# Queries and keys of one attention group as Strassen products, made before the pairs and loaded

## The chip, the cores and the metric

The kernel runs on one core of a Trainium2 chip, in a single launch. The metric is the device time of one execution in microseconds; the lower, the better. The time before is the median of three runs.

## The reference

A decoder trunk of two layers over x of 1024 rows and 1024 columns, in float32. The first layer is dilated sliding-window attention; the change touches only how its queries and keys are made. The second is a state-space layer (S5) with its own projections, a scan, and a gated linear unit.

```python
def dilated_attention_mixer(h, w_in, w_out, rel_bias):
    proj = h @ w_in
    qkv = proj[..., :n_qkv].reshape(B, S, 3, N_GROUPS_A, ATTN_HEADS, HEAD_DIM)
    z = proj[..., n_qkv:]
    for g, (window, dilation) in enumerate(DILATED_GROUPS):   # (128, 1), (512, 4), (2048, 16)
        o, l = dilated_group_attention(qkv[:, :, 0, g], qkv[:, :, 1, g], qkv[:, :, 2, g],
                                       rel_bias, window, dilation)
        ...
    wts = jax.nn.softmax(jnp.stack(lses), axis=0)
    o = jnp.sum(wts[..., None] * jnp.stack(outs), axis=0)
    return (o * jax.nn.silu(z)) @ w_out
```

There are 16 heads of 64 columns and three groups. Each group has its own queries, keys and values, so the input projection has 3 x 3 x 1024 columns and another 1024 for the gate.

## The kernel before, in words

Every large product is made of three TensorE matmuls: each operand is split into a high part (a float32r copy, made by ScalarE's cast) and a low part (the difference, made by VectorE or GpSimd), and high x high, high x low and low x high are added in PSUM. `split` does that; the tiles whi and wlo are the parts of a weight, hh and hl those of the normed input h, kept in SBUF as two halves of 512 rows.

**The values stage** (`v_phase`). The normed input is made and transposed. Chunk 0 of the values is a direct product (`first_values`). The other five chunks go through `Quads`: the input's four quarters (two halves of rows, two of the inner dimension) and their Strassen-Winograd sums are made once (`self.rows`), and each chunk of weights is cut in four quarters. `quad` runs seven products instead of eight: for each it makes the weight combination on VectorE (line 300), splits it, runs the matmuls, and adds the result into sums in SBUF (lines 337 to 348). Products that share an accumulator follow one another in one PSUM bank set (`ACC`). One product of the values is 48 matmuls with 256 moving columns (line 371). The results are stored to a DRAM tensor, v_dr. Between products, jobs for the second layer's tables run (`Prep.powers`, `Prep.products`), each after a given count of products, `q.jobs`: for table et of eight, powers after product 8 + 3 et and products after 10 + 3 et. Powers builds two tables in the two buffers of the ring wraw, and they stay there until products has used them.

**The pairs** (`attention`, `attn_pair`). Eight pairs of heads follow. In each, for each of the three groups, the query and then the key weights (128 columns each) are loaded (`load_w`, line 95) through the ring wraw, split into the rings whi and wlo (two buffers each; here GpSimd makes the low part, line 84), and multiplied with the two halves of h (`proj_half`, line 110: 24 matmuls of 128 x 512 each, into one of two PSUM banks psj). `evac_q` and `evac_k` split each result from PSUM into qh, ql, kh and kl, reordered so that the rows of a residue class of the dilation lie together. Each of these has a ring of two buffers, so group n + 2 takes the buffers of group n. Then `attn_unit` runs twice: scores (line 469) into psl, of which there is one, scaled bias and row maximum on VectorE (line 475), exponentials on ScalarE (line 486), transposes on TensorE (line 497), a split, and the product with the values vs (lines 546, 572). GpSimd merges the three outputs of the pair before and makes rotation tables for the second layer (`rotations`).

The rest is the attention's gate and output projection, the second layer with its projections, the gated linear unit, and the last projection.

The order of instructions on each engine is set at build time by a scheduler that knows dependencies and a model of costs; `high_priority(AHEAD)` lets an instruction go ahead of those emitted up to 600 places earlier. On the chip each engine runs its queue in that order. All DMAs of this kernel are issued from SP's queue.

Of the kernel before, what the change touches and what calls it, by code (L numbers as in the profile page):

```python
# [23 lines left out]
P = 128  # L24
S = 1024
# [2 lines left out]
H = 512  # L28
NEG = -1.0e30
EPS = 1e-6  # L30

AHEAD = 600

# [208 lines left out]
class Quads:  # L242
# [4 lines left out]
    def __init__(self, c):  # L247
        nc = c.nc
        self.c = c

        def part(th, kh):
            return [t[:, 4 * kh:4 * kh + 4, :] for t in c.h[th]]

        add, sub = ALU.add, ALU.subtract

        def tt(o, x, y, op):
            nc.vector.tensor_tensor(o, x, y, op=op)

# [24 lines left out]
        t2, t3 = c.vslot(2, F32), c.vslot(3, F32)  # L283
        self.sums = [t2[:, 0:2], t2[:, 2:4], t3[:, 0:2]]
        self.tmp = t3[:, 2:4].rearrange("p a x -> p (a x)")


    done, jobs = 0, {}

    def quad(self, raw, order, product, banks, use):  # L290

        c, nc = self.c, self.c.nc
        b11, b12, b21, b22 = raw
        n = b11.shape[2]
        tmp = self.tmp[:, 0:4 * n].rearrange("p (k x) -> p k x", k=4)
# [24 lines left out]

        accs = [None] * 3
        for i in order:
            w = weights(i)
            if accs[ACC[i]] is None:
                accs[ACC[i]] = banks(ACC[i])
            acc = accs[ACC[i]]
            product(i, self.rows[i], w, acc)
            self.done += 1  # L330
            for job in self.jobs.get(self.done, ()):
                job()
            with c.tc.high_priority(AHEAD):
                for b, ps in enumerate(acc):
                    p1, u2, u3 = (self.at(s, b) for s in self.sums)
                    if i == 0:
                        nc.scalar.copy(p1, ps)
                    elif i == 1:
                        t = c.slot("c11", tag="a")
                        nc.scalar.copy(t, ps)  # L340
                        use(0, 0, b, t)
                    elif i == 5:
                        nc.vector.tensor_tensor(u2, p1, ps, op=ALU.add)
                    elif i == 6:
                        nc.vector.tensor_tensor(u3, p1, ps, op=ALU.add)
                    else:
                        t, th, nh = {4: (u3, 1, 1), 3: (p1, 1, 0), 2: (u2, 0, 1)}[i]
                        nc.vector.tensor_tensor(t, t, ps, op=ALU.add)
                        use(th, nh, b, t)
# [30 lines left out]
        self.quad(quarters, [0, 1, 5, 6, 4, 3, 2], product, banks, use)  # L380


def gates(c, a, h, es):

    nc = c.nc
# [14 lines left out]
def v_phase(c, a, rows):  # L400
# [107 lines left out]
def out_tile(c, g, O):  # L508

    if not c.compact:  # L510
        c.compact = [c.outs.tile([64] + s, F32, name=f"cm{n}")
                     for n, s in enumerate(([3, 2, 32], [3, 32], [2, 32]))]
    if len(O) == g:
        O.append(c.outs.tile([P, S], F32, tag="O", name=f"O{g}", bufs=4))
    return O[g]


# [118 lines left out]
    return w  # L636


def attn_pair(c, p, w_in, h):
    nc = c.nc  # L640
    c.pair = p
    O = []
    for g in range(3):
        qh = c.attn.tile([P, S], F32R, tag="qh", name="qh", bufs=2)
        ql = c.attn.tile([P, S], F32R, tag="ql", name="ql", bufs=2)
        w = load_w(c, w_in[g * 8 + p])
        for th in range(2):
            src = proj_half(c, w, h[th])
            with c.tc.high_priority(AHEAD):
                evac_q(c, src, g, th * H, (qh, ql))  # L650
        bt = load_bias(c, p, g)
        kh = c.attn.tile([P, S], F32R, tag="kh", name="kh", bufs=2)
        kl = c.attn.tile([P, S], F32R, tag="kl", name="kl", bufs=2)
        w = load_w(c, w_in[(3 + g) * 8 + p])
        for th in range(2):
            src = proj_half(c, w, h[th])
            with c.tc.high_priority(AHEAD):
                evac_k(c, src, g, th * H, (kh, kl))
        v = load_v(c, p, g)
        rotations(c, p, g)  # L660
        if g == 1:
            run_merge(c)
        ms = c.small.tile([P, 32], F32, tag="ms", name="ms")
        for u in range(2):
            attn_unit(c, g, u, (qh, ql), (kh, kl), v, bt, ms, O)
            if p and g == u == 0:
                merge_weights(c, p - 1)
    if p == 7:
        merge_weights(c, p)
# [440 lines left out]
class Prep:  # L1110
# [4 lines left out]
    def __init__(self, c, a, v):  # L1115
        nc = c.nc
        self.c, self.a = c, a
        O = []
        o = [out_tile(c, c_, O) for c_ in range(4)]
# [319 lines left out]
def trunk(tc, a):  # L1439
# [4 lines left out]
    with ExitStack() as es:  # L1444
# [15 lines left out]
        dram = lambda name, shape: c.dr.tile(shape, F32, name=name)  # L1460
        c.vec_dr = dram("vec_dr", [3, 16, 384])
        c.v_dr = dram("v_dr", [3, 2, S, H])
        c.ms_dr = dram("ms_dr", [8, 3, 4, S])
        c.wt_dr = dram("wt_dr", [8, 3, 2, S])
        c.on_dr = dram("on_dr", [8, P, S])
# [139 lines left out]
```

## Time and profile before

| | |
|---|---|
| median of 3 runs | 1699.68 us (1697.64 to 1700.20) |
| profiled execution | 1703.36 us, span 1701.6 us, granted clock 0.992 |
| TensorE busy (PE) | 1651.8 us, 97% of the span, 9710 matmuls |
| TensorE weight loads (PEld) | 1399.3 us |
| VectorE (DVE) | 1012.8 us, 60% |
| ScalarE (ACT) | 711.9 us, 42% |
| GpSimd (POOL) | 461.6 us, 27% |
| DMA | 212.72 MB, mean 125 GB/s |

Busy time is the union of an engine's instruction times. A matmul's time in the profile reaches over the start of the next one, so TensorE's share says that it had work, and the distance from start to start says what a matmul costs. A row of a group of instructions has its line, engine, operation, tiles (written <- read) and shapes, its count, busy us and mean ns, and then the engine's idle time just before it and what ended that. In a timeline the idle time stands in brackets at the end of a row. A row of waits has the waiting engine and line, what it waited for, us in total, times and the longest. SPq is SP's DMA queue.

### The profile page before, as it was taken

Reading aid. Unit: us, or ns where it says so; the run is one execution under the profiler, and the core shown is the slowest. Engines: PE = TensorE matmul, PEld = TensorE weight load, DVE = VectorE, ACT = ScalarE, POOL = GpSimd, SP = SyncE. Lnnn points to the kernel's source line nnn. Section 1 sums busy time; section 2 is a strip of 40 time slices with the busy share of each in tenths; the row PEclk is TensorE's granted clock in tenths of the full one; section 3 lists DMA queues with packets and bytes.
Section 4 is the critical chain, followed back from the end, with each engine's and each line's share of the span. In section 5 each row is a group of like instructions: output and inputs, shape, how many; then the busy total and the mean of one; then the engine's idle time right before and its main releaser. Section 6 shows DMA issues by size and latency. Waiting matters only on the chain. (4 is left out here: it accounts for less than half of the span.)

```text
span 1701.6 us, 26274 instructions
## 1 busy us (share of the span) xinstructions
PE 1651.8 (97%) x9710; PEld 1399.3 (82%) x9710; DVE 1012.8 (60%) x2501; ACT 711.9 (42%) x1728; POOL 461.6 (27%) x303
## 2 busy tenths in 40 slices
PE   6999999999999999999999999998998999979998
PEld 5889999988888888888888888887887888868886
DVE  7698898725455455555455454558462777765533
ACT  5232232226556454645546464654452232233411
POOL 2000000041242513324161532404220444423121
PEclk9999999999999999999999999998999999999999
DMA  6223465352232323223242323428249765455432
GB/s 236 92 52 106 138 178 160 106 160 63 66 102 80 107 64 107 73 81 99 70 130 67 111 82 93 122 63 215 95 139 251 219 211 213 144 183 170 148 118 87
DMA packets 176901, 212.72 MB, mean 125 GB/s; under 512 B 37361, under 2 KB 133380, under 8 KB 176772
## 3 DMA queue, kind: packets, MB, share of 16 engines
q1 hardware_dynamic: 176772, 211.04, 41.4%
q8 instruction: 76, 1.25, 0.3%
q14 instruction: 53, 0.43, 0.1%
HBM read 154.03 MB, written 56.96 MB: 124 GB/s over the span
## 5 line engine op out<-in xcount | busy, mean ns | idle before, releaser
L110 PE MATMUL psj<-hh,whi 128*128 128x512 f32 x896 | 359.7, 401 | 3.4 <-DVE tz L784 3.4
L110 PE MATMUL psj<-hh,wlo 128*128 128x512 f32 x896 | 359.6, 401 | 0.0
L110 PE MATMUL psj<-hl,whi 128*128 128x512 f32 x896 | 356.3, 398 | 0.0
L84 POOL TENSOR_TENSOR wlo<-wraw,whi 128x1024 fp32r<-128x1024 f32 x48 | 115.2, 2399 | 392.7 <-ACT whi L83 329.1
L110 PEld LDWEIGHTS psj<-hh,whi 128*128 128x128 f32 x896 | 169.7, 189 | 40.4 <-DVE tz L784 3.8
L110 PEld LDWEIGHTS psj<-hh,wlo 128*128 128x128 f32 x896 | 169.5, 189 | 36.8 <-POOL wlo L84 0.3
L110 PEld LDWEIGHTS psj<-hl,whi 128*128 128x128 f32 x896 | 169.6, 189 | 36.3
L486 ACT ACTIVATE lg<-lg,nm 128x128 f32<-128x128 f32 (+1 forms) x384 | 168.2, 443 | 36.3 <-DVE nm L481 36.3
L83 ACT CAST whi<-wraw 128x1024 fp32r<-128x1024 f32 x80 | 83.7, 1047 | 195.6 <-PE psj L110 133.9
L475 DVE CUSTOM_DVE_ANT_0 lg<-psl,T 128x128 f32<-128x128 f32 (+1 forms) x384 | 110.6, 347 | 89.8 <-PE psl L469 89.8
L110 PE MATMUL psj<-h1h,whi 128*128 128x512 f32 (+1 forms) x272 | 106.0, 390 | 10.3 <-DVE z L1385 8.8
L371 PE MATMUL psq<-whi,v 128*128 128x256 f32 x640 | 115.9, 281 | 0.0
L84 DVE TENSOR_TENSOR ph<-pt,ph 128x512 fp32r<-128x512 f32 (+2 forms) x160 | 96.8, 623 | 15.5 <-ACT ph L83 13.4
L110 PE MATMUL psj<-h1h,wlo 128*128 128x512 f32 (+1 forms) x272 | 104.4, 385 | 0.0
L110 PE MATMUL psj<-h1l,whi 128*128 128x512 f32 (+1 forms) x272 | 104.2, 383 | 0.0
L84 DVE TENSOR_TENSOR kl<-psj,kh 128x512 fp32r<-128x512 f32 x48 | 33.2, 692 | 117.2 <-ACT kh L83 116.7
L83 ACT CAST ph<-pt 128x512 fp32r<-128x512 f32 (+2 forms) x160 | 81.6, 530 | 46.4 <-PE pt L497 45.3
L371 PEld LDWEIGHTS psq<-whi,v 128*128 128x128 f32 x640 | 98.6, 189 | 1.0 <-ACT whi L83 0.6
L371 PE MATMUL psq<-wlo,v 128*128 128x256 f32 x320 | 90.0, 282 | 2.2 <-DVE wlo L84 2.2
L546 PE MATMUL pso<-ph,vs 128*128 128x256 f32 (+1 forms) x544 | 86.5, 284 | 0.0
L1201 POOL TENSOR_TENSOR Ks<-Ks,O 32x64 f32<-32x64 f32 x8 | 4.6, 574 | 296.5 <-ACT Ks L1199 280.8
L497 PE MATMUL pt<-identr,lg 128*128 128x128 f32 x560 | 82.2, 277 | 0.0
(278 smaller groups left out, 3700.4 us busy)
## 6 DMA issues: line engine op xcount, KB each, us to landing
wraw<-in_w_in_dram SPq DMA_DIRECT2D x56, 512.0 KB
mw<-wt_dr SPq DMA_DIRECT2D x48, 256.0 KB
v<-in_w_v_dram SPq DMA_DIRECT2D x20, 512.0 KB
vp<-v_dr SPq DMA_DIRECT2D x16, 512.0 KB
wraw<-in_ssm_w_in_dram SPq DMA_DIRECT2D x16, 512.0 KB
v_dr<-v SPq DMA_DIRECT2D x30, 256.0 KB
rot_dr<-rt SPq DMA_DIRECT2D x48, 128.0 KB
ca_dr<-ca SPq DMA_DIRECT2D x32, 144.0 KB
```

What stands on the lines that cost most here:

```text
L83: nc.scalar.copy(hi, src)
L84: return (engine or nc.vector).tensor_tensor(lo, src, f32(hi), op=ALU.subtract)
L110: nc.tensor.matmul(ps, a[:, s], b[:, k, :], start=first and k == 0 and n == 0, stop=k == KT - 1 and n == 2, skip_group_check=True)
L371: nc.tensor.matmul(o, r[x][:, k, ts], w[y][:, k, :], skip_group_check=True, start=i in (0, 4, 5) and t % 2 == k == n == 0, stop=k == 3 and ...
L475: nc.vector.tensor_tensor_reduce(lg[:, h, j, 0:w], psl[:, h, o], bt[:, h, 256 - w:256], scale=1.0, scalar=-3.0e38, op0=ALU.add, op1=ALU.ma ...
L486: nc.scalar.activation(lg[:, h, j, 0:w], lg[:, h, j, 0:w], AF.Exp, bias=nm[:, h, b:b + 1], accum_out=ms[:, col:col + 1])
L497: c.nc.tensor.transpose(pt[:, n * P:(n + 1) * P], lg[:, h, j, part * P:part * P + P], c.ident)
L546: nc.tensor.matmul(o, l, r, start=n == 0, stop=n == len(jobs) - 1, skip_group_check=True)
L1201: nc.gpsimd.tensor_tensor(Ks[:, :, 0:16], Ks[:, :, 0:16], self.dd, op=ALU.add)
```

## The change

The queries and keys of the group with dilation 4 (g = 1) are no longer projected within the pairs. For each of the eight pairs, a new quad runs at the end of `v_phase`, behind the values. Its weights are the pair's 128 query columns and 128 key columns side by side, so that one half of the Strassen columns gives the queries and the other the keys. Its products have the weights as the stationary operand: 12 matmuls of 128 x 512 each. The raw weights alternate between two slots of the values stage, as do the sums (`self.turn`). Each result is split into its high and low part, reordered as the evacuation did it, and stored to a new DRAM tensor, qk_dr. The split parts stand in a buffer of the ring wraw, for the last two pairs in the ring b. In a pair the second group loads its four tiles from qk_dr into the buffers of the rings qh, ql, kh and kl.

The table jobs come after products 8 + 5 et and 11 + 5 et. `GROUPS` gives the order of the groups in a pair, which stays 0, 1, 2; `rotations`, `run_merge` and the merge's weights are called by place in that order.

```diff
+GROUPS = ((0, 1, 2), (0, 1, 2))
+MADE = [(p, 1) for p in range(8)]
...
+def halves(c, last, src, scale=None):
+    if last:
+        hi, lo = (c.slot(x, F32R, tag="b") for x in ("qkh", "qkl"))
+    else:
+        t = c.wraw.tile([P, 2, H], F32R, tag="wraw", name="qks")
+        hi, lo = t[:, 0], t[:, 1]
+    hi, lo = (x.rearrange("p (r l) -> p r l", r=src.shape[1]) for x in (hi, lo))
+    split(c, hi, lo, src, scale)
+    return hi, lo
+
+def put_qk(c, i, th, nh, t):
+    p, g = MADE[i]
+    o = ORD[g]
+    n = H // o
+    src, scale, at = t.rearrange("p (l r) -> p r l", r=o), None, th * n
+    if nh == 0:
+        src, scale, at = src[:, :, ::-1], 0.125, (1 - th) * n
+    for x, v in enumerate(halves(c, i >= len(MADE) - 2, src, scale)):
+        off = c.qk_dr.offset + ((i * 2 + nh) * 2 + x) * P * S + at
+        c.nc.sync.dma_start(bass.AP(c.qk_dr.tensor, off, [[S, P], [S // o, o], [1, n]]), f32(v))
...
+    def tiles(self, srcs, use):
+        c, nc = self.c, self.c.nc
+        self.turn ^= 1
+        raw = c.vslot(10 + self.turn, F32).rearrange("p (n a) x -> p n (a x)", n=2)
+        for n, s in enumerate(srcs):
+            nc.sync.dma_start(raw[:, n], s)
...
+        def product(i, r, w, acc):
+            for k in range(4):
+                for n, (x, y) in enumerate(((0, 0), (0, 1), (1, 0))):
+                    nc.tensor.matmul(acc[0], w[x][:, k, :], r[y][:, k, :], skip_group_check=True,
+                                     start=i in (0, 4, 5) and k == n == 0, stop=k == 3 and n == 2)
...
+        self.quad(quarters, [0, 5, 1, 6, 4, 3, 2], product, banks, lambda th, nh, b, t: use(th, nh, t))
...
-        q.jobs.setdefault(8 + 3 * et, []).append(lambda et=et: prep.powers(et))
-        q.jobs.setdefault(10 + 3 * et, []).append(lambda et=et: prep.products(et))
+        q.jobs.setdefault(8 + 5 * et, []).append(lambda et=et: prep.powers(et))
+        q.jobs.setdefault(11 + 5 * et, []).append(lambda et=et: prep.products(et))
     for ch in range(2, 6):
         q.values(a, ch)
+    for i, (p, g) in enumerate(MADE):
+        q.tiles([a["w_in"][(3 * x + g) * 8 + p] for x in range(2)],
+                lambda th, nh, t, i=i: put_qk(c, i, th, nh, t))
...
+def queries_keys(c, p, g, w_in, h):
+    q, k = ([c.attn.tile([P, S], F32R, tag=x + y, name=x + y, bufs=2) for y in "hl"] for x in "qk")
+    if (p, g) in MADE:
+        for n, ts in enumerate((q, k)):
+            for x, t in enumerate(ts):
+                c.nc.sync.dma_start(f32(t), c.qk_dr[MADE.index((p, g)), n, x])
+        return q, k
+    for n, (ts, evac) in enumerate(((q, evac_q), (k, evac_k))):
+        w = load_w(c, w_in[(3 * n + g) * 8 + p])
...
+    for n, g in enumerate(GROUPS[p % 2]):
+        q, k = queries_keys(c, p, g, w_in, h)
```

More of the change, by code (lines that the diff above doesn't have):

```diff
@@ L285, in __init__ @@
         self.tmp = t3[:, 2:4].rearrange("p a x -> p (a x)")
+        self.turn = 0
     done, jobs = 0, {}
@@ L380, in values, with banks @@
         self.quad(quarters, [0, 1, 5, 6, 4, 3, 2], product, banks, use)
+    def tiles(self, srcs, use):
[4 more added lines that the diff above has]
+            nc.sync.dma_start(raw[:, n], s)
+        raw = raw.rearrange("p n (k x) -> p n k x", k=KT)
+        quarters = [raw[:, nh, 4 * kh:4 * kh + 4] for kh in range(2) for nh in range(2)]
+        def banks(n):
+            pool, tag = ((c.psj, "psj"), (c.psl, "psl"), (c.pso, "pso"))[n]
+            return [pool.tile([P, H], F32, tag=tag, name="psq")]
+        def product(i, r, w, acc):
[3 more added lines that the diff above has]
+                                     start=i in (0, 4, 5) and k == n == 0, stop=k == 3 and n == 2)
+        turn = self.turn
+        self.at = lambda s, b: s[:, turn]
+        self.quad(quarters, [0, 5, 1, 6, 4, 3, 2], product, banks, lambda th, nh, b, t: use(th, nh, t))
 def gates(c, a, h, es):
@@ L649, in attn_pair @@
             with c.tc.high_priority(AHEAD):
-                evac_q(c, src, g, th * H, (qh, ql))
-        bt = load_bias(c, p, g)
[L652 to L658, printed above, removed]
+                evac(c, src, g, th * H, ts)
+    return q, k
+def attn_pair(c, p, w_in, h):
+    c.pair = p
+    O = {}
+    for n, g in enumerate(GROUPS[p % 2]):
+        q, k = queries_keys(c, p, g, w_in, h)
+        bt = load_bias(c, p, g)
         v = load_v(c, p, g)
-        rotations(c, p, g)
-        if g == 1:
+        rotations(c, p, n)
+        if n == 1:
             run_merge(c)
@@ L664, in attn_pair @@
         for u in range(2):
[L665 to L666 removed]
+            attn_unit(c, g, u, q, k, v, bt, ms, O)
+            if p and n == u == 0:
                 merge_weights(c, p - 1)
@@ L1117, in __init__ @@
         self.c, self.a = c, a
-        O = []
-        o = [out_tile(c, c_, O) for c_ in range(4)]
+        O = {}
+        o = [out_tile(c, n, O) for n in range(4)]
         def table(t, at, w):
```

15 lines of the change are left out of this document (4 added, 11 removed).

## The prediction

> **What bounds the kernel now.** I read the page's engine totals first, then the stretches, TensorE's waits, and the timeline. The columns of a stretch are its length, busy us and instruction count of each engine, the granted clock, the DMA share and GB/s. 113 to 343 us is the values stage, 343 to 1170 us the eight pairs, 560 to 657 us one pair.
>
> ```profile
> PE 1651.8 (97%) x9710; PEld 1399.3 (82%) x9710; DVE 1012.8 (60%) x2501; ACT 711.9 (42%) x1728; POOL 461.6 (27%) x303
> ...
> 113.00:343.00 230.00, 226.18 (x1882) 217.53 (x1881) 190.94 (x411) 62.12 (x96) 9.79 (x16) 1.00 0.44 135
> 343.00:1170.00 827.00, 823.61 (x4967) 684.55 (x4966) 421.66 (x1289) 438.11 (x1259) 281.48 (x150) 1.00 0.34 96
> ...
> 560.00:657.00 97.00, 97.00 (x598) 80.83 (x597) 49.50 (x158) 52.48 (x154) 34.38 (x18) 1.00 0.31 87
> ```
>
> TensorE is busy without a break in both stages; VectorE has 83% of the values stage (190.9 of 230 us) and about half of a pair. The two views of TensorE's waits, of the values stage and of 345 to 1160 us, have little:
>
> ```profile
> PE psq L371 <- DVE wlo L84: 3.0, 2, 2.2
> ...
> PE psj L110 <- DVE tz L784: 3.4, 1, 3.4
> ```
>
> So time taken off TensorE comes off the span, as long as its cover holds. But a busy matmul overlaps the next, so its price is not the 401 ns of its row but the distance of starts. The first projections of the pairs run 99 matmuls unbroken, from the first to the last of these:
>
> ```profile
> 344.20 0.39 PE L110 MATMUL psj<-hh,whi 128*128 128x512 f32 x1
> ...
> 366.97 0.39 PE L110 MATMUL psj<-hl,whi 128*128 128x512 f32 x1
> ...
> 345.00:365.00 20.00, 20.00 (x88) 16.23 (x87) 1.00 0.66 196
> ```
>
> 22.77 us over 98 distances is 0.2324 us; 20 us over the 87 weight loads gives 0.230. I use 0.2324.
>
> The Trainium skill, "TensorE: Matmul & The Clock Gate", section Back-to-back issue gap, gives about 131 ns for a sustained 512-column matmul with its weight load; the sum's first term would then be 96 x 0.131 = 12.6 us and the time about 1693. The trace has 232 ns for these very matmuls, so that gets no chance of its own.
>
> **TensorE.** For each of eight pairs the second group's queries and keys are now 2 weights x 2 halves x 8 k x 3 = 96 matmuls of 128x512, 22.31 us. As one quad they are 7 products x 4 x 3 = 84 of the same shape, 2.79 us a product, 19.52 us a quad. Saved: 96 matmuls, 22.3 us. That moves eight quads (156 us) behind the values and leaves each pair 97.0 - 22.3 = 74.7 us.
>
> **VectorE and ScalarE in the quads.** The rows nearest to the new operations:
>
> ```profile
> L348 DVE TENSOR_TENSOR v<-v,psq 128x512 f32<-128x512 f32 x29 | 19.8, 685 | 9.9 <-PE psq L371 9.7
> ...
> L1224 DVE TENSOR_TENSOR ca<-ca,O 128x576 f32<-128x576 f32 x8 | 6.5, 814 | 0.0
> L1228 DVE SCALAR_TENSOR_TENSOR ca<-ca,O 128x576 f32<-128x576 f32 x8 | 6.0, 755 | 0.1
> L1230 DVE TENSOR_TENSOR zi<-zi,O 128x512 f32<-128x512 f32 x8 | 5.5, 689 | 0.1
> ...
> 300.04 0.39 DVE L1186 COPY O<-zi 64x64 f32<-64x64 f32 x2
> ...
> L87 DVE SCALAR_TENSOR_TENSOR ql<-psj,qh 128x512 fp32r<-128x512 f32 x48 | 32.7, 680 | 68.3 <-ACT qh L86 68.3
> L84 DVE TENSOR_TENSOR kl<-psj,kh 128x512 fp32r<-128x512 f32 x48 | 33.2, 692 | 117.2 <-ACT kh L83 116.7
> L86 ACT ACTIVATE qh<-psj 128x512 fp32r<-128x512 f32 x48 | 28.2, 588 | 14.1 <-PE psj L110 14.1
> L83 ACT CAST whi<-wraw 128x1024 fp32r<-128x1024 f32 x80 | 83.7, 1047 | 195.6 <-PE psj L110 133.9 <-issue 35.7 <-DMA wraw<-in_ssm_w_in_dram 16.3
> L84 POOL TENSOR_TENSOR wlo<-wraw,whi 128x1024 fp32r<-128x1024 f32 x48 | 115.2, 2399 | 392.7 <-ACT whi L83 329.1
> ```
>
> A quad has 20 VectorE operations of 512 elements (4 subtractions, 7 low parts of weights, 5 sums, 4 low parts of results): 20 x 0.69 = 13.8 us. ScalarE has 7 casts, 2 copies, 4 high parts: 13 x 0.59 = 7.7 us. Both lie beside 19.5 us of products. The table jobs, now every 5 products instead of 3, reach into the first two quads with the powers of two tiles. One is 6 operations on 576 elements, 6 on 512 and 4 small copies (0.19 each): 6 x 0.77 + 6 x 0.69 + 0.8 = 9.5 us. VectorE in the quads: 8 x 13.8 + 19 = 129 of 156 us, 83%, what the values stage has now.
>
> The tightest path: the whi/wlo ring holds two, so the weights of product n start when product n-2 ends and have 2.79 us. Cast 0.59 and low part 0.69 leave 1.5 us, two VectorE operations ahead in the queue (the sum of n-2, and one under way). It fits, with less room than the values' products have (48 matmuls each). Where it fails, TensorE is late next. Bounds: 0, and VectorE as the pace of the first two quads at its 83%, (13.8 + 9.5)/0.83 = 28.1, twice 8.6 over, 17 us. I take 2 us, the values' 3.0 us scaled by 156/230, which has the same load. The first projection after the last quad needs cast 1.05 and GpSimd's 2.40 in 2.79 us: 0.7 us, taken as 1.
>
> **Stored halves and the queue.** Six quads put their split results into the two wraw buffers, four a quad, each with two stores from SP. Rows: a store's issue (ns, least/median/most) and two stretches of the values stage; then, from the page, the DMA share and rate of forty slices.
>
> ```profile
> L377 SPq DMA_DIRECT2D v_dr<-v x30: 359/381/1163, 141.8 to 344.3; - x30
> ...
> 220.00:260.00 40.00, 39.66 (x331) 37.88 (x331) 36.22 (x58) 11.89 (x20) 1.56 (x4) 1.00 0.55 165
> 260.00:300.00 40.00, 39.28 (x325) 37.23 (x324) 32.30 (x48) 11.54 (x20) 2.28 (x4) 1.00 0.55 165
> ...
> DMA  6223465352232323223242323428249765455432
> GB/s 236 92 52 106 138 178 160 106 160 63 66 102 80 107 64 107 73 81 99 70 130 67 111 82 93 122 63 215 95 139 251 219 211 213 144 183 170 148 118 87
> ```
>
> A quad reads 1 MB and writes 2 MB: 3.1 MB in 19.5 us is 161 GB/s, as now at 220 to 300 us; 251 have been reached. SP issues 10 DMAs, 3.8 us. A buffer is held for 0.59 + 0.69 + 0.76 + 0.5 MB at 165 GB/s (3.2) = 5.2 us; four a quad on two buffers is 10.4 of 19.5 us: hidden. In the first two quads the powers' tables hold both buffers from their job to the products job three products later, 8.4 us, and a result waits. If its cast stands at the head of ScalarE's queue, the weights' casts behind it wait, and TensorE after them. Bounds 0 and 2 x 8.4 = 17; I take 2, near 0, since the sums alternate and nothing else needs the result. A store on SP waits for VectorE's low part, with the next raw loads queued behind it; raws alternate too, so a load has nearly a quad of slack: nothing.
>
> **The values stage** has 17 us less table work on VectorE. Its 3.0 us of waits may go, or others come with the new order: -3 to +2, I take -1.
>
> **The pairs.** VectorE loses 4 x 0.69, ScalarE 4 x 0.58 and 2 x 1.05, GpSimd 2 x 2.4: 46.7, 48.1 and 29.6 us in 74.7, at most 64%. SP issues four loads of 512 KB instead of two, 0.7 us more. They wait for the buffers of the pair before's third group, that is for its last scores, and hold back what is queued behind them on SP: the values (vp), the bias (T), the weights (wraw), the merge's rows. SP stands like that today:
>
> ```profile
> SPq L95 <- POOL wlo L84: 155.3, 38, 11.5
> ```
>
> Between those scores and the second group's first ones lie the first group's projections, 22.3 us, and its scores; 2 MB at the pair's 87 GB/s is 24 us, at 251 it is 8. I count nothing; if the cover is gone it is up to 10 us a pair, inside the next bound.
>
> What is lost is TensorE's filler. Scores start where the first four rows say; the fifth counts projections between them; the last three are VectorE's waits there.
>
> ```profile
> 565.25 0.39 PE L469 MATMUL psl<-kl,qh 64*128 64x256 f32 x2
> 572.63 0.39 PE L469 MATMUL psl<-kl,qh 64*128 64x256 f32 x2
> 579.76 0.39 PE L469 MATMUL psl<-kl,qh 64*128 64x256 f32 x2
> 593.31 0.39 PE L469 MATMUL psl<-kl,qh 64*128 64x256 f32 x2
> ...
> 565.25:593.31 28.06, 22.04 (x91) 1.00 0.43 120
> ...
> 573.43 0.69 DVE L87 SCALAR_TENSOR_TENSOR ql<-psj,qh 128x512 fp32r<-128x512 f32 x1 [3.22 <-ACT qh L86]
> 580.28 0.69 DVE L84 TENSOR_TENSOR kl<-psj,kh 128x512 fp32r<-128x512 f32 x1 [4.59 <-ACT kh L83]
> 587.58 0.69 DVE L84 TENSOR_TENSOR kl<-psj,kh 128x512 fp32r<-128x512 f32 x1 [4.03 <-ACT kh L83]
> ```
>
> The first group's two units take 28 us with 91 projection matmuls between. With the second group loaded, what is ready there is the third's: two psj banks, 48 matmuls, until the first group's scores free its q and k buffers. At the old spacing (91 - 48) x 0.2324 = 10 us a pair would be idle, 80 in all. But VectorE idles 3 to 5 us in each spacing of 7, waiting only for evacuated projections, so the scores can follow one another faster, and loaded ones can move up. Bounds 0 and 80; I take 2 for the eight, by these idle rows.
>
> **Sum**, against the profiled execution's 1703.4 us: -22.3 + 2 + 1 + 2 - 1 + 2 = -16.3, so 1687.1. The median of the runs, 1699.7, is 3.7 lower: 1683.
>
> **Rivals.** (1) Slower: the filler is missed, in the first group of each pair. Without that term the change gains 18.3 us, so it decides at 18.3/8 = 2.3 us of idle a pair; with half the spacing kept, 5 us a pair, the time is 1683 - 2 + 40 = 1721; fully kept, 1761. For it: the 10 us above. Against: VectorE's idle rows. One row shows what such a hole does to the clock:
>
> ```profile
> 1070.00:1170.00 100.00, 96.61 (x559) 80.38 (x558) 61.57 (x154) 56.12 (x158) 25.20 (x14) 0.97 0.47 129
> ```
>
> 3.4 us without a matmul and a granted clock of 0.97 where the stretches before had 1.00. The Trainium skill, "TensorE: Matmul & The Clock Gate", section on the clock gate, lets a hole of about 3.4 us halve the clock until it is busy again; this row agrees, and by it, 3.4 us at half speed or 1.7 us for one hole in each pair, 1721 would get 14 us more.
>
> (2) No change, or a part of the gain: the quads are paced by VectorE and the buffers, not TensorE. Both upper bounds together are 17 + 17 instead of 4, 1683 + 30 = 1713; half of that, 1698, is the likelier end. For it: 2.79 us is a short turn for two queues in order. Against: the average load is no higher than now.
>
> (3) More than forecast: nothing new waits and the values' waits go: 1699.7 - 22.3 - 3 = 1674. That the change doesn't remove the matmuls can't be: their count is in the code.
>
> **Chances.** Forecast, 1674 to 1693: 0.61. (3), below 1674: 0.06. (2): 0.19, of which 0.09 ends at 1693 to 1696, 0.09 within 0.2% (3.4 us, about what a measurement of this kernel can tell from no change), 0.01 above. (1): 0.14, of which 0.01 is within 0.2%. So faster 0.76, same 0.10, slower 0.14. Leaving out 0.05 below and 0.13 above gives 1672 to 1704; the forecast's own range is 1674 to 1693.
>
> **What would show it.** Right: 672 matmuls of 128x512 at the new products, starts 0.232 us apart, in a stage of 156 to 163 us behind the values; psj matmuls of the pairs fewer by 768, pairs 75 to 76 us apart; TensorE's waits in both stages a few us. Wrong: TensorE waiting for whi or wlo, or for the SP queue, in the quads (2); score matmuls waiting for the loaded q or k, or transposes for ScalarE's exponentials, with a clock below 1.00 in the pairs (1).

## The result, and the profile after

The changed kernel takes 1749.01 us (median of 4 runs, 1748.07 to 1750.06) against 1699.94 us: a ratio of 1.0291, with a 95% interval of 1.0273 to 1.0309. It is 49 us slower; 1683 was forecast, in a range of 1674 to 1693. The mean granted TensorE clock is 0.974, before 0.992.

The page after, its line of engine totals and the granted clock in forty slices:

```profile
PE 1654.7 (95%) x9614; PEld 1401.0 (80%) x9614; DVE 1110.0 (63%) x2629; ACT 752.1 (43%) x1784; POOL 429.5 (25%) x287
...
PEclk9999999999998999999999999999999999999999
```

TensorE has 96 instructions less (768 matmuls of 512 columns out, 672 in) and is still busy 1654.7 us, before 1651.8. An engine whose busy time doesn't fall when its work does is slowed or held up, and the totals don't say where. The stretches do. Columns: stretch, length, busy us and instructions of TensorE, its weight loads, VectorE, ScalarE and GpSimd, granted clock, DMA share, GB/s. First the kernel before: from the first scores to the last product with the values (the eight pairs), one pair, and the rest to the last product.

```profile
371.00:1145.10 774.10, 774.10 (x4766) 645.25 (x4766) 397.25 (x1253) 418.71 (x1221) 259.39 (x136) 1.00 0.31 87
759.50:856.60 97.10, 97.10 (x600) 80.91 (x599) 49.69 (x158) 52.57 (x153) 34.36 (x19) 1.00 0.31 88
...
1145.10:1693.00 547.90, 523.18 (x2500) 434.32 (x2500) 327.48 (x628) 180.37 (x340) 168.88 (x134) 0.98 0.56 170
```

The same view of the kernel after: the quads, the pairs, one pair, two pieces of that pair, and the rest.

```profile
328.40:499.00 170.60, 166.06 (x746) 132.31 (x745) 126.79 (x186) 81.96 (x118) 4.51 (x6) 1.00 0.53 156
528.40:1183.00 654.60, 622.16 (x4009) 524.47 (x4008) 384.02 (x1217) 381.09 (x1172) 223.66 (x119) 0.96 0.38 111
851.60:933.70 82.10, 77.44 (x504) 65.43 (x503) 46.76 (x153) 47.77 (x148) 29.64 (x16) 0.96 0.40 116
866.20:871.20 5.00, 0.70 (x11) 0.37 (x7) 3.12 (x12) 3.44 (x8) 2.34 (x1) 0.80 0.27 67
869.20:876.00 6.80, 4.82 (x28) 4.70 (x29) 6.40 (x29) 4.81 (x18) 0.27 (x1) 0.50 0.32 96
...
1183.00:1739.60 556.60, 522.69 (x2490) 432.84 (x2489) 322.60 (x632) 181.00 (x342) 167.93 (x134) 0.98 0.56 169
```

The last product of the Strassen stage ends at 499.0 us where the values ended at 342.9: 156.1 us later. The first scores follow 29.4 us behind it, before 28.1. The pairs take 654.6 us instead of 774.1, 119.5 less, and the rest 8.7 more: 156.1 + 1.3 - 119.5 + 8.7 = 46.6 us, the distance of the two profiled executions' last products.

A pair takes 82.1 us, not 74.7. Two places in it show why: 5.0 us in which TensorE has 0.70 us of work, and, from inside that hole on, 6.8 us at half clock. In the first row of before, TensorE had work in all of 774.10 us, at clock 1.00.

### The profile page after: what moved, and what is told of

It is laid out like the page before. It is cut to its first block, busy times and chain, and to the rows that moved or that the text cites. A ratio compares the mean times of both kernels' runs of the same rounds, so it can differ in the third digit from the quotient of the medians.

```text
span 1748.2 us, 26671 instructions
## 1 busy us (share of the span) xinstructions
PE 1654.7 (95%) x9614; PEld 1401.0 (80%) x9614; DVE 1110.0 (63%) x2629; ACT 752.1 (43%) x1784; POOL 429.5 (25%) x287
## 3 DMA queue, kind: packets, MB, share of 16 engines
q8 instruction: 75, 1.23, 0.3%
## 5 line engine op out<-in xcount | busy, mean ns | idle before, releaser
L114 PE MATMUL psj<-hh,whi 128*128 128x512 f32 x640 | 257.2, 402 | 7.3 <-DVE tz L845 6.4
L114 PE MATMUL psj<-hl,whi 128*128 128x512 f32 x640 | 256.2, 400 | 0.0
L114 PE MATMUL psj<-hh,wlo 128*128 128x512 f32 x640 | 255.0, 399 | 0.0
L88 POOL TENSOR_TENSOR wlo<-wraw,whi 128x1024 fp32r<-128x1024 f32 x32 | 76.6, 2394 | 380.4 <-ACT whi L87 364.6
L87 ACT CAST whi<-v 128x512 fp32r<-128x512 f32 (+1 forms) x91 | 71.4, 786 | 182.0 <-PE psq L401 91.9
L114 PEld LDWEIGHTS psj<-hh,whi 128*128 128x128 f32 x640 | 121.5, 190 | 33.7 <-DVE tz L845 6.6
L114 PEld LDWEIGHTS psj<-hh,wlo 128*128 128x128 f32 x640 | 121.1, 189 | 25.6 <-POOL wlo L88 0.2
L114 PEld LDWEIGHTS psj<-hl,whi 128*128 128x128 f32 x640 | 121.3, 190 | 25.3
L604 PEld LDWEIGHTS pso<-ph,vs 128*128 128x128 f32 x544 | 83.7, 208 | 20.5 <-ACT ph L87 10.7
L88 DVE TENSOR_TENSOR wlo<-v,whi 128x512 fp32r<-128x512 f32 (+1 forms) x91 | 81.3, 893 | 24.9 <-ACT whi L87 24.3
```

Source lines behind the costliest of these rows:

```text
L87: nc.scalar.copy(hi, src)
L88: return (engine or nc.vector).tensor_tensor(lo, src, f32(hi), op=ALU.subtract)
L114: nc.tensor.matmul(ps, a[:, s], b[:, k, :], start=first and k == 0 and n == 0, stop=k == KT - 1 and n == 2, skip_group_check=True)
L604: nc.tensor.matmul(o, l, r, start=n == 0, stop=n == len(jobs) - 1, skip_group_check=True)
```

## What stands in the hole

TensorE's weight loads, by what they waited for in the pairs, before and after (us in total, times, longest):

```profile
PEld psl L469 <- issue: 22.2, 66, 0.4
PEld psl L469 <- DVE cm L610: 2.6, 7, 0.4
```

```profile
PEld psl L527 <- DVE ms L533: 23.1, 15, 2.9
PEld psl L527 <- issue: 14.1, 46, 0.4
PEld pso L604 <- ACT ph L87: 10.7, 7, 1.9
```

The first and the last line of after are new at this size: scores that wait for VectorE's score reduction to free psl, and products that wait for ScalarE's cast of the transposed exponentials (ph). The first comes 15 times in the eight pairs, the other 7 times. One such place in TensorE's timeline of after (start, us, what, idle before it in brackets):

```profile
865.60 0.19 PEld L527 LDWEIGHTS psl<-kl,qh 64*128 64x128 f32 x2 [0.60 <-DVE ms L533]
...
868.07 0.19 PEld L604 LDWEIGHTS pso<-ph,vs 128*128 128x128 f32 x1 [1.71 <-ACT ph L87]
871.18 0.29 PEld L527 LDWEIGHTS psl<-kl,qh 64*128 64x128 f32 x2 [2.93 <-DVE ms L533]
```

ScalarE and VectorE at the same time:

```profile
866.02 1.03 ACT L87 CAST whi<-wraw 128x1024 fp32r<-128x1024 f32 x1
866.96 0.50 ACT L544 ACTIVATE lg<-lg,nm 128x256 f32<-128x256 f32 x1
867.37 0.19 ACT L544 ACTIVATION_READ_ACCUMULATOR lg<-lg,nm 128x1 f32 x1
867.46 1.04 ACT L87 CAST ph<-pt 128x512 fp32r<-128x512 f32 x2
870.05 0.28 ACT L671 ACTIVATE cm<-cm 64x96 f32<-64x96 f32 x1 [1.55 <-DVE cm L670]
870.24 1.05 ACT L90 ACTIVATE qh<-psj 128x512 fp32r<-128x512 f32 x2
```

```profile
862.54 1.23 DVE L88 TENSOR_TENSOR vs<-vp,vs 128x1024 fp32r<-128x1024 f32 x1 [0.26 <-ACT vs L87]
...
865.12 0.42 DVE L533 CUSTOM_DVE_ANT_0 lg<-psl,T 128x256 f32<-128x256 f32 x1
865.47 0.08 DVE L533 DVE_READ_ACCUMULATOR2_ANT ms<- 128x1 f32 x1
868.01 1.51 DVE L668 TENSOR_TENSOR cm<-cm 64x32 f32<-64x32 f32 x1 [2.46 <-DMA cm<-ms_dr]
869.55 0.18 DVE L669 TENSOR_TENSOR cm<-cm,cm 64x32 f32<-64x32 f32 x1
...
869.95 0.41 DVE L533 CUSTOM_DVE_ANT_0 lg<-psl,T 128x256 f32<-128x256 f32 x1
```

Two queues in order explain both waits. On ScalarE the cast of a weight's high part (whi), sent ahead by `high_priority`, stands before the casts of ph that TensorE needs; up to there ScalarE works without a break, so nothing in its idle time hints at it. On VectorE three small operations of the merge (cm) stand before the score reduction that frees psl, and the first of them waits 2.46 us for a DMA. The reduction of the scores that started at 865.60 could have begun some 3 us earlier: on TensorE they took 0.9 us, and it began at 869.95. The merge's wait goes on to ScalarE: its exponential stands there for 1.55 us, ahead of the evacuation of the third group's queries (qh), without which the banks psj aren't free for further projections.

None of these queue entries is new, and neither is the DMA's wait. Before, VectorE waited 18.6 us in all for it, now 13.5, and in the pair shown

```profile
758.59 0.83 DVE L610 TENSOR_TENSOR cm<-cm 64x32 f32<-64x32 f32 x1 [2.52 <-DMA cm<-ms_dr]
```

But there it stood ahead of the pair's first score reduction, and the scheduled order now has it ahead of the fourth. The load itself comes later in the pair: SP issued it 3.3 us before the pair's first score, and issues it 12.9 us behind it now. What is new besides is what TensorE has beside these entries. The projections' weight loads (psj) in the first two pieces of this pair:

```profile
851.60:862.70 11.10, 5.11 (x28) 1.00 0.15 44
862.70:876.00 13.30, 0.00 (x0) 0.74 0.34 94
```

and in the corresponding stretch of the kernel before:

```profile
759.50:787.00 27.50, 16.51 (x90) 1.00 0.43 123
```

Before, 90 projection matmuls lay between the pair's first score and its fifth, so that such waits passed unseen. Now there are 28, and for 13.3 us none.

## The experiments

Each ratio is to the kernel before on the same chip (1701.6 to 1704.6 us), with its 95% interval. Differences to the change are taken from the medians; by the ratios they come out 0 to 6 us larger. The length of the pairs is counted as above, from the first score to the last product with the values.

**1. Is it the stage or the pairs?** (e3) The quads run and store as in the change, and no pair uses them.

```diff
-    if (p, g) in MADE:
+    if p > 7:
```

> The quads run and store their results, but no pair loads them: all pairs project their second group as before (the quads' work is done twice over, the output is the same). It prices the stage by itself. Both theories, which put the loss in the pairs: before + 156 to 162, so 1856 to 1862. If instead the quads cost more than their products (the prediction's second rival), 1870 or more.

Measured: 1863.31 us, 1.0938 (1.0912 to 1.0963), 159 us over the kernel before. One pair of it:

```profile
723.50:820.60 97.10, 97.10 (x598) 80.90 (x597) 49.68 (x157) 52.58 (x153) 34.40 (x18) 1.00 0.32 88
```

The pairs are those of before. The stage costs what was forecast for it (156.2 + 2 + 1 + 2 - 1 = 160), so the second rival, quads paced by VectorE and the buffers, is out; the loss is in the pairs.

**2. Half of the pairs.** (e4) `MADE = [(p, 1) for p in range(0, 8, 2)]`.

> Only pairs 0, 2, 4 and 6 have quads and load; the others project. Half of the change: four quads at 20 us against 22.3 us, so -9 us, and three pairs (2, 4, 6) whose start has both the merge's wait and no projections. Theory A: three holes of 7 us, 1700 - 9 + 21 = about 1712. Theory B (each made pair loses as much, the first included): 1724, half way.

Measured: 1728.79 us, 1.0147 (1.0125 to 1.017). Starts of pairs lie 79.3, 100.5, 80.8, 100.9, 77.5, 99.8 and 76.3 us apart: pairs that load give less than the 22.3 us, and those between them, which project all, are about 3 us longer than the 97.1 of before. This is near theory B. Loss goes with the number of loaded groups; two pairs in a row aren't needed for it.

**3. The merge's place, moved in the program.** (e1) The merge's weights are called one unit later.

```diff
-            if p and n == u == 0:
+            if p and n == 0 and u == 1:
```

> The merge's weights of the pair before are put behind the first group's second unit instead of its first; nothing else differs from the changed kernel. Theory A (head of the queue): in the changed kernel the first merge operation (cm) stands at the head of VectorE's queue waiting for its DMA, the score reductions of the second unit stand behind it, psl stays full, and TensorE, which has no projections there any more, idles and falls to half clock. Then this edit gives most of the 7 us a pair back: pairs about 76 us apart instead of 82, no half-clock stretch per pair, time 1695 to 1710. Theory B (thin filler): the first group's chain of scores, exponentials and transposes is too long for the projections that are left, whatever stands in it. Then the time stays at 1740 to 1750 and the holes stay at the same place.

Measured: 1749.03 us, 1.0266 (1.0242 to 1.029). The scheduler put the merge's operations at the same place in VectorE's queue, ahead of the fourth reduction, and the run says nothing on the merge.

**4. Its place, forced.** The same call one unit later, but queued behind the last score reduction of that unit (e5a), or behind the last split of its exponentials (e5b).

```diff
+            if p and n == 0 and u == 1:
+                with c.tc.issue_after(c.last_lg):
+                    merge_weights(c, p - 1)
```

In e5b `c.last_ph` stands in place of `c.last_lg`.

> The merge's weights of the pair before are queued behind the last score reduction of the first group's second unit on VectorE (an order edge, no wait); moving the call alone had left VectorE's order as it was. Theory A (merge at the head of VectorE's queue): the score reductions no longer stand behind the DMA, the 3 us hole and the half clock after it go, pairs 76 to 78 us apart instead of 82, time 1700 to 1715. Theory B (thin filler): holes of the same total appear a little later, 1740 to 1750.

> As the run before, but behind the last split of the first group's exponentials (ph), some 10 us later in VectorE's queue, where the DMA has landed long before. Theory A: no wait for the merge's rows at all, pairs 75 to 77 us apart, time 1690 to 1710; the merge itself on GpSimd ends later and might hold the next output buffer, then 1715. Theory B: 1740 to 1750.

Measured: 1737.26 us, 1.0223 (1.0195 to 1.025), and 1760.68 us, 1.0336 (1.03 to 1.0372). Behind the scores the new wait shrinks, and the other stays:

```profile
PEld pso L604 <- ACT ph L87: 11.4, 7, 1.7
PEld psl L527 <- DVE ms L533: 8.2, 10, 1.8
```

23.1 us have become 8.2 and the time is 12 us less, so the cm wait ahead of the scores costs about that. The time lies between the two theories' ranges: the wait is real, and most of the loss is not it. Farther back the merge is too late for others: products wait for the outputs' buffers there, up to 3.4 us at once.

**5. Another order of groups.** `GROUPS = ((0, 2, 1), (0, 2, 1))`, so that the loaded group comes last (e2), and the same with the merge behind the split of the exponentials (e6).

> The groups run in the order first, third, second in every pair, so that the loaded group is the last and the third group's projections stand behind the first group. Theory A: the merge's wait is now covered by the third group's projections; pairs 75 to 77 us apart, time 1690 to 1705. Theory B: the hole only moves, to the third group, which has no projections behind it but those of the next pair's first group; 1735 to 1755.

> Order first, third, second, and the merge's weights behind the last split of the first group's exponentials. Theory A: the loaded group is last, each group's chain has projections beside it, and the queue is free: 1683 to 1700, better than order 0, 1, 2. Theory B: no better than the same order without the edge, 1735 to 1748.

Measured: 1741.24 us, 1.0227 (1.0179 to 1.0274), and 1764.71 us, 1.0362 (1.0338 to 1.0387). In e2 the first two pairs take 70.1 and 74.7 us, the first of them without a merge before it; from the third on they take 79 to 86. That is theory B's range. The holes move, they don't close: VectorE waits 21.2 us in 7 pairs for the merge's rows, where the change has 12.9. e6 lies above both ranges, as e5b does, and why is not taken apart.

**6. The merge's rows from an older pair.** (e7) The rows of pair p - 2 are loaded instead of p - 1, so that the DMA need not wait for fresh ones.

```diff
-    src = bass.AP(c.ms_dr.tensor, c.ms_dr.offset + p * 3 * 4096, [[32, 64], [2048, 6], [1, 32]])
+    src = bass.AP(c.ms_dr.tensor, c.ms_dr.offset + of * 3 * 4096, [[32, 64], [2048, 6], [1, 32]])
```

> The merge's operations stay at the call's old place, but they read the rows of the pair two before, which landed long ago (so the outputs are weighted with another pair's rows): the DMA's wait is gone, the work is not. Theory A: 1695 to 1712, and VectorE waits for the merge's load in the first pairs alone. Theory B: 1740 to 1750.

Measured: 1770.61 us, 1.0406 (1.039 to 1.0422). The load itself came to stand later in SP's queue, behind loads of values; VectorE waited 15.3 us in 7 pairs for it, no less than the change's 12.9. The edit didn't take away what it was to take away, and the run decides nothing between the theories.

**7. The merge's parts left out.** In pairs 0 to 6: weights and GpSimd's sum (e8), the sum alone (e9), the weights alone (e10, where the sum reads other rows).

> The changed kernel without the merge of pairs 0 to 6: neither the merge's weights (VectorE, ScalarE, their DMAs) nor the three-way sum on GpSimd; the third group's raw output is stored in its place. Theory C (the merge in the shorter pairs: VectorE held by it, by its DMA or by GpSimd's long operations): every pair then looks like the first one, which has no merge and took 77.2 us where the others take 82; six pairs x 4.9 give 1749 - 29 = 1720 or less, and holes only as in the first pair. Theory B (thin filler, the merge has nothing to do with it): 1740 to 1750.

> Only GpSimd's three-way sum of pairs 0 to 6 and the loads for it are left out; the merge's weights are still made on VectorE and stored. If theory C holds by GpSimd's operations holding VectorE's (two operations of the changed kernel ran 1.5 and 2.3 us where 0.2 is usual, while GpSimd ran): 1725 to 1735. If it holds by the wait for the merge's DMA: no change, 1745 to 1750. Theory B: no change.

> Only the merge's weights of pairs 0 to 6 are left out, with their DMAs; GpSimd's sum runs with rows loaded from another stored tensor. If theory C holds by the wait for the merge's DMA at the head of VectorE's queue: 1720 to 1730. If by GpSimd: 1740 to 1750. Theory B: 1740 to 1750.

Measured: 1729.01 us, 1.0161 (1.0146 to 1.0176); 1748.9 us, 1.0274 (1.0257 to 1.0291); 1745.11 us, 1.0254 (1.0238 to 1.0269). The whole merge accounts for 20 us, each half alone for 0 to 4. So the merge is a part of the loss, less than the 29 us of theory C. Without the sum the cm wait is where it was. Without the weights the sum starts earlier and gets in VectorE's way, as the timelines of VectorE and GpSimd in e10 show at one place:

```profile
783.33 3.28 DVE L88 TENSOR_TENSOR vs<-vp,vs 128x1024 fp32r<-128x1024 f32 x1 [0.26 <-ACT vs L87]
786.64 0.42 DVE L533 CUSTOM_DVE_ANT_0 lg<-psl,T 128x256 f32<-128x256 f32 x1
```

```profile
783.15 2.38 POOL L743 TENSOR_TENSOR O<-O,mw 128x1024 f32<-128x1024 f32 x1 [10.90 <-DVE O L635]
785.61 5.67 POOL L745 TENSOR_TENSOR O<-O,O 128x1024 f32<-128x1024 f32 x2
```

The subtraction of vs, 1.23 us in the change's row above, takes 3.28: it ends 1.08 us after GpSimd's first operation does. The median of all 24 such subtractions is 3.18 us in e10 and 1.23 in the change, so e10 puts a new cost in the place of the one it takes away and doesn't price the DMA's wait. The Trainium skill, "SBUF — State Buffer", section Who interferes with whom, says that a VectorE instruction with two inputs in SBUF contends with a GpSimd instruction that reads SBUF, and calls the contention an exclusive lock; these rows agree.

**8. Low parts of the pairs' weights on VectorE.** (e11) Without `c.w_engine = nc.gpsimd`.

> The low parts of the pairs' weights (wlo) on VectorE instead of GpSimd: four operations of 1.2 us a pair on VectorE instead of four of 2.4 us on GpSimd. If GpSimd's operations hold VectorE's at the hole: 1735 to 1742 in spite of 5 us more VectorE work a pair. If not, VectorE is later everywhere: 1750 to 1765.

Measured: 1740.14 us (1736.72 to 1747.17), 1.023 (1.0202 to 1.0258). Some 9 us come back; from the second pair on, starts lie 78.2 to 84.6 us apart. It fits the lock above, and shows it for no single place.

**9. ScalarE's chain or missing filler?** e12 takes the cast of whi off ScalarE; e13 and e14 leave these queue entries and put other matmuls, those of the attention's gate with their casts and tanh, beside them (their results take the ring a there); e15 adds the merge's new place to e14.

The new lines of e12, which hold where GpSimd makes the low part:

```diff
+            nc.vector.tensor_copy(hi, raw)
+            c.last_lo = c.w_engine.tensor_tensor(lo, raw, f32(hi), op=ALU.subtract).ins
```

Those of e13:

```diff
-    gates(c, a, c.h, range(EARLY, 8))
...
+        if n == 1 and p % 2 == 0:
+            gates(c, dict(w_in=w_in), h, [EARLY + p // 2])
```

Those of e14 and e15:

```diff
-    gates(c, a, c.h, range(EARLY, 8))
...
+        if n == 1:
+            gates(c, dict(w_in=w_in), h, [EARLY + p // 2], [p % 2])
```

> In the pairs the high parts of the projections' weights are copied by VectorE instead of ScalarE (a copy of 128x1024, about 1 us, moves from one engine to the other; nothing else changes). ScalarE's chain as the cause: the hole between the two groups of a pair closes by the 1 us to 3 us that the cast takes ahead of the exponentials' casts, 8 to 24 us in all, 1725 to 1738. Missing filler as the cause: ScalarE's place in it is taken by the next wait, VectorE gets the same work, 1745 to 1755.

> The gates of the last four blocks (48 matmuls of 128x512 each, about 11.2 us) leave the values stage and are issued ahead of the second group of pairs 0, 2, 4 and 6. No matmul is added or removed and no wait is taken away. Missing filler as the cause: in these four pairs the half clock and the hole go, they take 82 - 7.3 + 11.2 = 86 us, the other four stay at 82, the values stage loses 45 us: 1749 - 4 x 7.3 = 1720. ScalarE's chain or VectorE's queue as the cause: these pairs take 82 + 11 = 93 us and the time stays at 1749; it is worse if the gates' tanh on ScalarE lengthens the chain.

> The same four gates in halves: 24 matmuls (5.6 us) ahead of the second group of every pair, each gate's weights loaded and split twice. Missing filler as the cause: 5.6 us of matmuls nearly cover the 5.2 us of TensorE idle in each pair and the half clock behind it goes: pairs of 82 - 7.3 + 5.6 = 80 us and 45 us less in the values stage, 1749 - 8 x 5 to 7 = 1693 to 1709. Waits in the queues as the cause: pairs of 87 to 88 us, 1745 to 1755.

> As the run before, with the merge's weights queued behind the last score reduction of the first group's second unit (which by itself gave 1737, 12 us less). If filler and the merge's place are two causes that add: about 12 us below the run before, 1683 to 1697. If they are one and the same (a wait that counts only where no filler stands beside it): no more than 3 us from the run before.

Measured: 1733.06 us, 1.0164 (1.0136 to 1.0192); 1736.48 us, 1.0188 (1.0173 to 1.0204); 1739.07 us, 1.0194 (1.0175 to 1.0214); 1721.93 us, 1.0104 (1.008 to 1.0129).

e12 falls into the range of ScalarE's chain. Its pairs as a whole, and one of them:

```profile
527.80:1164.30 636.50, 617.73 (x4007) 518.88 (x4007) 400.22 (x1245) 357.31 (x1144) 231.88 (x119) 0.97 0.39 115
...
766.70:840.30 73.60, 72.21 (x483) 60.60 (x482) 48.83 (x156) 44.08 (x142) 30.69 (x16) 1.00 0.42 124
```

18 us less in the pairs, although VectorE got the copies, 16 us more work. One pair of eight takes 73.6 us, no more than forecast.

e13's sum came out far from its forecast, for a reason outside the pairs. The values stage between 80 and 120 us, one pair with a whole gate, and all pairs:

```profile
80.00:120.00 40.00, 22.75 (x145) 22.26 (x146) 38.70 (x125) 9.95 (x9) 0.00 (x0) 0.70 0.08 25
668.60:755.40 86.80, 86.80 (x563) 72.86 (x562) 49.24 (x156) 51.56 (x153) 34.53 (x18) 1.00 0.42 117
510.70:1170.70 660.00, 649.53 (x4199) 543.98 (x4199) 374.09 (x1224) 390.88 (x1183) 238.11 (x123) 0.99 0.41 117
```

The gates had been covering VectorE's preparation of the quads there, and the stage gave back 17 us (its end went from 499.0 to 481.7), not 45. In the pairs the filler did what was expected of it: 45 us of matmuls added and only 5.4 us more time, 660.0 against 654.6; in the pair shown, no hole and full clock. So 39 us of room stood empty in the pairs. The mistake in the expectation was the price of the place that the filler was taken from.

e14 lies between its two forecasts: the stage gives back 17.5 us there, not 45, and a pair takes about 83 us, not 80. All pairs take 663.2 us, 8.6 more than the change's, for the same 45 us of added matmuls.

e15 is 17 us under e14, where moving the merge alone gave 12: the two add. Its pairs:

```profile
509.70:1159.40 649.70, 645.50 (x4201) 541.01 (x4200) 390.51 (x1225) 396.66 (x1188) 240.45 (x127) 1.00 0.42 122
```

They hold 45 us more matmuls than the change's and take 4.9 us less. The clock is full, and TensorE is without work for 4.2 us in all, where the change has 32.4. With other matmuls beside the chain and the merge behind the scores the holes are gone; against 774.1 - 178.5 + 44.6 = 640.2 us the pairs are 9.5 us over. Most of what the time still lacks is in the stage that gave the gates away.

**10. Both waits out of the way.** e16 is e12 with e5a; e17 has also the last two gates, in halves, in pairs 1, 3, 5 and 7.

```diff
+        if n == 1 and p % 2:
+            gates(c, dict(w_in=w_in), h, [EARLY + 2 + p // 4], [p // 2 % 2])
```

> The high parts' copies on VectorE and the merge's weights behind the last score reduction, together. Two causes that add: 16 + 12 = 28 us less, 1721, pairs of about 76 to 77 us. One and the same wait seen twice: no more than the larger one, 1733, pairs of 78 us.

> As the run before, and the gates of the last two blocks leave the values stage and stand in halves ahead of the second group of pairs 1, 3, 5 and 7. In the run with four whole gates the values stage gave back only 18 of the 45 us of moved matmuls (TensorE busy 22.75 of 40 us between 80 and 120 us, beside a VectorE busy 38.70). With two gates left there the stage should give back about 17 of 22 us, and the pairs should take the 4 x 5.6 us in what is left of their holes: 1721 - 17 + 0 to 11 = 1704 to 1715. If the pairs have no holes left they grow by 22 us in all, and it is 1720 to 1727.

Measured: 1723.81 us, 1.0114 (1.01 to 1.0129), and 1716.17 us, 1.0071 (1.0056 to 1.0085). Their pairs, first e16's, then e17's:

```profile
529.10:1158.70 629.60, 614.36 (x4007) 514.80 (x4007) 396.81 (x1245) 357.16 (x1144) 230.98 (x119) 0.98 0.39 116
```

```profile
514.20:1151.60 637.40, 629.11 (x4104) 526.48 (x4104) 410.95 (x1253) 360.62 (x1148) 239.03 (x123) 0.99 0.41 119
```

16 and 12 us alone, 25 together: two causes that nearly add. e17 gives back 15 us ahead of the pairs and takes 22 us of matmuls for 8 us of time. It is the best version run, and 12 us slower than the kernel before.

## Why the prediction was wrong

**The step that failed** is the pairs' +2 us. Pairs of 74.7 us were forecast, 8 x 22.3 = 178.5 us less in all and 2 given back; they gave 119.5. That term is 59 us instead of 2, and the other differences are small beside it: 49 - (-17) = 66 us in the times. Two parts make up 54.7 of the 59: TensorE is without work for 654.60 - 622.16 = 32.4 us, and the clock is halved for 58.0 us, in 44.7 of which TensorE works, an estimated cost of half of that, 22.3.

The argument for 2 us was that VectorE idles 3 to 5 us in each spacing of the scores, "so the scores can follow one another faster". They do. The first and the fifth score of a pair, before:

```profile
759.45 0.39 PE L469 MATMUL psl<-kl,qh 64*128 64x256 f32 x2
...
787.51 0.38 PE L469 MATMUL psl<-kl,qh 64*128 64x256 f32 x2
```

and after:

```profile
851.58 0.39 PE L527 MATMUL psl<-kl,qh 64*128 64x256 f32 x2
...
871.18 0.58 PE L527 MATMUL psl<-kl,qh 64*128 64x256 f32 x2 [2.73 <-DVE ms L533]
```

28.1 us became 19.6, a gain of 8.5 where a pair has 22.3 us less to do; the pair as a whole gained 15.0. Idle rows and a load of "at most 64%" say how much an engine could do on average. They don't say in which order its queue holds it. The other half of the argument, 48 ready projections of the third group, counted what is there and not when it runs: in the pair shown 20 of them run before the first score, and only the 28 others stand between the scores. At the change from the first group to the second, ScalarE has outputs, exponentials and a weight cast in one unbroken row, and VectorE has a DMA's wait at its head.

**The first rival** is what happened, with a chance of 0.14. Its mechanism was the one named, filler missed in a chain without enough ready matmuls, and so was a clock below 1.00. The waits named for it were not: no score waits for a loaded q or k, and transposes wait 2.7 us in all for exponentials; scores wait for the score reduction and products for the cast of ph. Its place was one step later, where the first group's exponentials meet the second group's scores, and it lacked the queue entries that make the chain long. It was priced at 5 us a pair (1721, or 1735 with the clock) to 10 (1761); measured were 59/8 = 7.4 a pair. By the rows above, a pair's hole has 5.0 - 0.70 = 4.3 us without TensorE work, and the 4.82 us of work at half clock would have taken 2.4 less at full clock: 6.7 together. The prediction's 5 us of idle and 1.7 of clock come to the same 6.7, with the parts at 4.1 and 2.8 on the mean of the eight pairs (32.4/8 and 22.3/8). The clock's part was misread from its own row: 0.97 over 100 us is some 6 us at half clock behind one hole, not 3.4.

**The clock** behaves as the prediction's row had hinted. The Trainium skill, "TensorE: Matmul & The Clock Gate", section on the clock gate, has a half clock after an idle window of about 3.4 us. The trace agrees with the halving, to 0.50. It doesn't show an empty window of that length: the half clock begins at 869.18, in the second of the idle pieces of 1.71 and 2.93 us, and in the 3.41 us before that TensorE had work for 1.12. It stood for 6.8 us.

**Right:** the stage. The median distance of its matmuls' starts is 0.231 us. They come in five groups, of 256, 128 and three times 96, 672 in all (ns, least/median/most; the first and the last start); the first and the last of the groups:

```profile
L430 PE MATMUL psq<-v,whi x256: 387/394/502, 333.4 to 498.8; 128*128 128x512 f32 x128
...
L430 PE MATMUL psq<-hh,wlo x96: 388/393/505, 328.9 to 496.2; 128*128 128x512 f32 x96
```

The weight loads' waits for weights, in the view of 320 to 499 us, are

```profile
PEld psq L430 <- ACT whi L87: 3.4, 2, 2.0
PEld psq L430 <- DVE wlo L88: 3.1, 4, 1.4
```

That is 6.5 us; the matmuls themselves, whose 3.0 us of waits the prediction had scaled, wait 2.5 us there for whi and wlo, against 2 + 2. The stage with its handover came to 156.1 + 1.3 = 157.4 us against 160. Loading the stored parts is hidden too: TensorE's list of waits in the pairs names no loaded q or k. Three waits of its matmuls are put down there to the values' load (vp), 4.9 us in all; they stand at the same places as weight loads that wait for the cast of ph, so they are that wait.

**Not foreseen:** 8.7 us behind the pairs. 5.4 of them lie between the first matmuls of the second layer and its first scan product, a stretch with a DMA share of 0.94 (before 0.97). No experiment aimed there, and why it grew is open.

**Open** as well: e16's pairs still take 629.6 us, 34 more than 774.1 - 178.5. TensorE is without work in 629.60 - 614.36 = 15.2 of them, and 23.9 us at half clock cost some 12 more; its largest named wait is 6.8 us in all, and the remaining 7 us are not accounted for. e13 shows that filler closes such holes, and none was found that cost nothing where it came from. A version faster than before was not reached. What was not tried is weaving the loaded group's scores into the third group's projections by hand.

## What to carry to other kernels

Matmuls that an engine can do without are not always saved time: where independent matmuls stand between the steps of a dependent chain, they hide that chain's waits, and taking them out is worth only what the chain can be shortened by. Before removing filler, read the order of each other engine's queue at the place where it stood, for waits on a DMA at a queue's head and for work sent ahead by priority; average load and idle time say nothing on it. The same holds for an experiment that moves filler: price the place that it leaves.

## What the runs showed of the hardware that was not expected

A small VectorE operation can be held until a GpSimd operation ends. The merge's first operation on 64x32 elements took 1.51 us at 868.01, to 869.52, where the next one took 0.18; GpSimd's low part of a weight was running until 869.47:

```profile
867.13 2.34 POOL L88 TENSOR_TENSOR wlo<-wraw,whi 128x1024 fp32r<-128x1024 f32 x1 [16.34 <-ACT whi L87]
```

Over the eight pairs its median is 1694 ns, before 766. The score reductions, with one operand in PSUM, kept their 0.42 us beside GpSimd's two operations of 5.67 us together in e10.

Idle pieces that are each shorter than 3 us are followed by half clock, for 10.2 us in the change's first pair and for 6.8 in each of the others. In the pairs of all runs here a stretch of half clock lasts 3.4, 6.8, 10.2, 13.7 or 17.1 us, a multiple of 3.41. In the change the last seven begin 81.92 us apart, 24 times 3.413, where the pairs' starts lie 81.8 to 82.2 us apart; whether one sets the other is not shown.
